# Queries on the column halves as outer and middle 256, and one sum of exponentials instead of two in front of its product

## The chip, the core and the metric

The kernel runs on one core of a Trainium2 chip. The core has a matrix engine (TensorE, called PE; PEld is its loading of weights), VectorE (DVE), ScalarE (ACT), GpSimd (POOL) and SyncE (SP), each with a queue of its own that runs in order, and 16 DMA engines. The metric is the device time of one execution in microseconds (us); lower is better.

## The reference

One step of an encoder layer over 2048 prompt tokens and 32 sample tokens with a width of 1024. A combined projection gives the columns of three groups of heads: two recurrences, and a forgetting attention with 8 heads of 64 numbers. Their outputs are joined and go through an output projection; a feed-forward block with 2816 hidden numbers follows. All arrays are float32. The change is in the prompt's attention:

```python
s = jnp.einsum('bqhd,bkhd->bhqk', q, k) * FOX_SCALE
bias = jnp.swapaxes(c_q, 1, 2)[..., :, None] - jnp.swapaxes(c_k, 1, 2)[..., None, :]
s = jnp.where(k_pos[None, :] <= q_pos[:, None], s + bias, -jnp.inf)
return jnp.einsum('bhqk,bkhd->bqhd', jax.nn.softmax(s, axis=-1), v)
```

`c` is the running sum of the log forget values. A query sees the keys up to its own place.

## The kernel before

The prompt's attention is done in 32 *units*: one head `h` and one group `g` of 512 queries, with `g` from 0 to 3. A unit has two generators. `first` loads and splits queries and keys, and `shift` finds each query's largest score: matmuls L665 into a PSUM bank, maxima on DVE (L667, and L670 with a mask for the last piece), a small matmul L677 that turns them into a row, L680 and L681. `second` calls `values`, which the diff touches.

`values` goes over blocks of 128 keys, 4g+4 of them. For each, two matmuls (L728, L729) give the scores transposed, with keys on the partitions and 512 queries along the columns; the last four blocks are on the diagonal, where block j has no use for the first 128j queries (`c0`) and gets a mask added on DVE (L732). ACT takes the exponential (L738) into a tile `pt`; for the first two blocks this tile is one of two accumulators `acc[0]`, `acc[1]`. Four blocks at a time, `use` multiplies the value rows with `pt` (L712). The value block is 64 columns wide, half of PE's array, so the 512 queries are cut in two: x=0 is queries 0 to 255 and writes PSUM partitions 0 to 63, x=1 is queries 256 to 511 and writes partitions 64 to 127 of the bank `pv`. Each float32 matmul of this line appears in the trace as two rows with a weight load each. In the group with the diagonal the last block is multiplied first. In group 0, whose first four blocks are the diagonal, the order is that of the blocks. `use` also adds `pt` to the accumulator of the block's parity (L722), on POOL or DVE by the block's number (`FX_POOL`); the trace calls the accumulators `fx_acc`.

At the end `quotient` multiplies a matrix of ones with both accumulators (L827; four matmuls, each half accumulating over two), which puts each query's sum of exponentials on all 64 partitions. After that come a logarithm and an exponential on ACT (L832, L833), a product on DVE that reads the bank (L834), and two stores to the array `yT` from ACT's queue (L836), one per half. The output projection reads `yT` later.

The order in which generators advance is written out in `run` (a time for `first` and one for `second`, with a lead between them) and in `paced`, which mixes the attention with the other work: the last projection of the inputs and the loading of the output weights for group 0, then the output projection of the first four token tiles (L1739 to L1741) and the first feed-forward block (L1881 to L1883, L1831 to L1833), whose weights are cast on ACT (L1767) and split on POOL (L1768). With one `pv` bank, `run` finishes the unit's quotient at once, `drain(ends.pop(0))`; for some units of group 0 there are two banks and the quotient comes during the next unit. From this program the tile framework's planner makes the final order of each engine's queue ahead of time: it takes the earliest instruction whose inputs it reckons to be ready, and gives L712 a higher priority.

Of the kernel before, what the change touches and what calls it, by code (L numbers as in the profile page):

```python
# [12 lines left out]
AF = mybir.ActivationFunctionType  # L13
ALU = mybir.AluOpType
# [546 lines left out]
class Fox:  # L561
# [123 lines left out]
    def values(self, k, q, nq, blocks, vr, hc, dst, done, pp):  # L685

        nc, fp = self.K.nc, self.fp
        ka, kb = k  # L690
        qa, qb = q
        nx = 2 if nq > 256 else 1
        W = nq // nx
        pv = pp("pv")
        acc = [fp.tile([128, 512], F32, name=f"fx_acc{i}", bufs=2) for i in range(2)]
        last = len(blocks) - 1
        todo = []

        def use(n):


            now = [todo.pop(0) for _ in range(n)]
            opens = now[0][0] == 0
            order = now if opens and now[-1][2] else now[::-1]
            mms = [(i, m, pt, x, max(c0, W * x), W * x + W) for i, m, c0, pt in order for x in range(nx)]
            mms = [t for t in mms if t[4] < t[5]]
            left = [sum(t[3] == x for t in mms) for x in range(nx)]
            before = None
            with self.K.tc.high_priority():
                for i, m, pt, x, a, b in mms:  # L710
                    left[x] -= 1
                    mm = nc.tensor.matmul(pv[64 * x:64 * x + 64, a - W * x:W], lhsT=vr[:m, i, hc], rhs=pt[:m, a:b],  # L712
                                          start=(opens and i == order[0][0]), stop=(now[-1][0] == last and not left[x]),
                                          skip_group_check=True)
                    if before is not None:
                        self.K.tc.add_manual_dep(mm.ins, before.ins.name, mybir.DependencyInfo(
                            mybir.DependencyClass.NoSync, mybir.DependencyReason.DATA), reason="together")
                    before = mm
            for i, m, c0, pt in now:
                if i >= 2:  # L720
                    eng = nc.gpsimd if i % 8 in FX_POOL else nc.vector
                    eng.tensor_tensor(acc[i % 2][:m, c0:nq], acc[i % 2][:m, c0:nq], pt[:m, c0:nq], ALU.add)  # L722

        for i, (key, m, c0, diag) in enumerate(blocks):
            ks = slice(key, key + m)
            s0 = min(c0, max(0, nq - 256))
            ps = pp("ps")
            nc.tensor.matmul(ps[:m, s0:nq], lhsT=ka[:, ks], rhs=qa[:, s0:nq], start=True, stop=False)  # L728
            nc.tensor.matmul(ps[:m, s0:nq], lhsT=kb[:, ks], rhs=qb[:, s0:nq], start=False, stop=True)  # L729
            if diag:  # L730
                d = min(128, nq - c0)
                nc.vector.tensor_tensor(ps[:m, c0:c0 + d], ps[:m, c0:c0 + d], self.mask_t[:m, :d], ALU.add)  # L732
            pt = acc[i] if i < 2 else fp.tile([128, 512], F32, name="fx_pt", bufs=FX_PT)
            if i < 2 and c0:
                nc.gpsimd.memset(pt[:, :c0], 0.0)
            if i < 2 and m < 128:
                nc.gpsimd.memset(pt[:, :nq], 0.0)
            nc.scalar.activation(pt[:m, c0:nq], ps[:m, c0:nq], AF.Exp)  # L738
            todo.append((i, m, c0, pt))
            if len(todo) == FX_LAG + FX_TOGETHER:  # L740
                use(FX_TOGETHER)
            yield
        while todo:
            use(min(len(todo), FX_TOGETHER))
            yield
        done(self.quotient(acc, pv, nq, nx, dst))

    def sample(self, g, pp):

# [68 lines left out]
                            in_=r[:64, 128:256].rearrange("d (h t) -> d h t", h=4))  # L818
        yield

    def quotient(self, acc, pv, nq, nx, dst):


        nc, W = self.K.nc, nq // nx
        for i in range(2):
            for x in range(nx):
                nc.tensor.matmul(pv[64 * x:64 * x + 64, 256:256 + W], lhsT=self.ones, rhs=acc[i][:, W * x:W * x + W],  # L827
                                 start=(i == 0), stop=(i == 1), skip_group_check=True)
        yield
        r, P = acc[0], 64 * nx  # L830
        s = r[:P, 256:256 + W]
        nc.scalar.activation(s, pv[:P, 256:256 + W], AF.Ln)  # L832
        nc.scalar.activation(s, s, AF.Exp, scale=-1.0)  # L833
        nc.vector.tensor_tensor(r[:P, :W], pv[:P, :W], s, ALU.mult)  # L834
        for x in range(nx):
            nc.scalar.dma_start(out=dst(x), in_=r[64 * x:64 * x + 64, :W])  # L836

    def run(self, units, nk, slots, pp, lead):


        K, nc, fp = self.K, self.K.nc, self.fp
        vs, ks, ends = {}, {}, []
# [8 lines left out]
        def load_v(p):  # L851
            NB = nk // 128
            o = len(vs) % slots * NB
            vs[p] = self.vr[:, o:o + NB, :]
            nc.sync.dma_start(out=vs[p], in_=K.tm[:nk, 128 * p:128 * p + 128].rearrange("(b t) c -> t b c", t=128))
# [14 lines left out]
        def second(u, h, g):  # L870
            row, hc = 256 + 64 * h, slice(64 * (h % 2), 64 * (h % 2) + 64)
            if h // 2 not in vs:
                load_v(h // 2)
            blocks = [(128 * b, 128, max(0, 128 * b - 512 * g), b >= 4 * g) for b in range(4 * g + 4)]
            yield from self.values(ks[h], u["q"], 512, blocks, vs[h // 2], hc, lambda x: K.yT[
                row:row + 64, 512 * g + 256 * x:512 * g + 256 * x + 256], ends.append, pp)

        units = [(h, g, {"i": i}) for i, (h, g) in enumerate(units)]
        seen = set()
# [11 lines left out]
        while s < len(units):  # L891
            if gf is None and f < len(units) and s >= need[f]:
                h, g, u = units[f]
                gf = first(u, h, g)
            if gs is None and s < f:
                h, g, u = units[s]
                gs, k = second(u, h, g), 0
            if gs is None or (gf is not None and tf <= ts + lead):
                tf += FX_F
                if next(gf, StopIteration) is StopIteration:  # L900
                    gf, f = None, f + 1
            else:
                ts += 1.0
                k += 1
                if k > FX_END and ends and next(ends[0], StopIteration) is StopIteration:
                    ends.pop(0)
                if next(gs, StopIteration) is StopIteration:
                    gs, s = None, s + 1
                    while ends and len(pp.slots["pv"]) == 1:
                        drain(ends.pop(0))  # L910
            yield
# [1319 lines left out]
```

## Time and profile before

| what | us |
|---|---|
| three timed runs | 3605.97, 3607.12, 3612.27; median 3607.12 |
| the profiled execution, its own time | 3604.76 |
| its span, first to last instruction | 3603.0 |
| granted PE clock over the span | 0.976 of full |

The median of the runs is the time that counts. The trace is of the profiled execution; its span leaves out 1.8 us around the first and the last instruction. Times of day below are us from the span's start. "x" before a number is a count of instructions, and an arrow points at what an instruction writes, from what it reads.

### The profile page before, as it was taken

The page shows a single profiled execution, that of the slowest core. Times are in us where ns is not written, and L with a number is a line of the kernel's source. Part 1 is how long each engine was busy: PE and PEld are TensorE (multiplying, and loading weights), DVE is VectorE, ACT ScalarE, POOL GpSimd, SP SyncE. Part 2 cuts the span into 40 slices and gives each one's busy share as a digit, 9 for nine tenths or more (in the row PEclk, how much of TensorE's full clock was granted, in tenths as well). Part 3 has the DMA queues.
Part 4 walks back from the last instruction along what each step waited for, and adds up shares of the span by engine and source line. Part 5 has one row for each costly group of instructions (what it writes and reads, how often), then busy time and mean ns, then how long its engine had stood idle before and what let it go on. Part 6 is the DMA issues. An engine that isn't in the chain of part 4 may idle for free.

```text
span 3603.0 us, 60961 instructions
## 1 busy us (share of the span) xinstructions
PE 3408.2 (95%) x24106; PEld 2859.4 (79%) x24106; DVE 1883.4 (52%) x3855; ACT 1403.1 (39%) x2865; POOL 1371.8 (38%) x1458
## 2 busy tenths in 40 slices
PE   7999999999999989999999998999999999999999
PEld 5888898877778856666666666779999998998998
DVE  3466667656576555656656655533333344333336
ACT  4356456554555454444434433312222223111212
POOL 5434445434344314544444333333233243222223
PEclk9999999999999979999999999999999999999999
DMA  6433343425532453322222214533222232211212
GB/s 210 144 122 109 99 146 112 126 80 159 186 96 92 129 147 108 92 73 79 77 64 66 58 55 128 181 118 90 65 71 65 70 106 89 65 59 52 66 59 97
DMA packets 362481, 361.24 MB, mean 100 GB/s; under 512 B 35359, under 2 KB 304244, under 8 KB 361140
## 3 DMA queue, kind: packets, MB, share of 16 engines
q1 hardware_dynamic: 324336, 320.02, 29.2%
q10 hardware_dynamic: 37476, 37.29, 3.4%
q8 instruction: 189, 3.10, 0.4%
q14 instruction: 96, 0.79, 0.1%
q0 software_dynamic: 384, 0.05, 0.0%
HBM read 291.14 MB, written 66.14 MB: 99 GB/s over the span
## 4 chain that ended last, share of the span: by engine, by line
PE 61%; DVE 6%; POOL 4%; ACT 3%; DMA 3%; issue 3%; ACTq 0%; SPq 0%; POOLq 0%; DVEq 0%
PE ff_p L1883 8%; PE ff_p L1882 8%; PE ff_p L1881 8%; PE ff_o L1832 4%; PE ff_o L1833 4%; PE ff_o L1831 4%; PE pb_pv L712 4%; PE rw_ps L227 3%; PE pb_sc L665 2%; PE pb_ps L728 2%; PE op_p L1740 1%; PE op_p L1739 1%; PE op_p L1741 1%; PE pb_ps L729 1%; PE ip_p L378 1%
## 5 line engine op out<-in xcount | busy, mean ns | idle before, releaser
L1882 PE MATMUL ff_p<-h_lo,wih 128*128 128x384 f32 (+2 forms) x1760 | 623.0, 354 | 0.1
L1883 PE MATMUL ff_p<-h_hi,wil 128*128 128x384 f32 (+2 forms) x1760 | 621.4, 353 | 1.1 <-POOL wil L1768 1.1
L1881 PE MATMUL ff_p<-h_hi,wih 128*128 128x384 f32 (+2 forms) x1760 | 620.7, 353 | 1.4 <-DVE op_r L1743 0.4
L1768 POOL TENSOR_TENSOR wil<-ff_st,wih 128x1024 fp32r<-128x1024 f32 x134 | 322.4, 2407 | 579.9 <-ACT wih L1767 546.6
L378 PE MATMUL ip_p<-h_hi,w_hi 128*128 128x256 f32 (+1 forms) x1472 | 454.8, 309 | 22.4 <-DVE ip_e L343 9.6
L379 PE MATMUL ip_p<-h_lo,w_hi 128*128 128x256 f32 (+1 forms) x1472 | 423.5, 288 | 5.1 <-POOL h_lo L203 2.0
L380 PE MATMUL ip_p<-h_hi,w_lo 128*128 128x256 f32 (+1 forms) x1472 | 423.4, 288 | 0.4 <-POOL w_lo L336 0.4
L1881 PEld LDWEIGHTS ff_p<-h_hi,wih 128*128 128x128 f32 x1760 | 331.2, 188 | 17.3 <-DVE ff_sg L1812 0.8
L1883 PEld LDWEIGHTS ff_p<-h_hi,wil 128*128 128x128 f32 x1760 | 333.0, 189 | 14.4 <-POOL wil L1768 1.4
L1882 PEld LDWEIGHTS ff_p<-h_lo,wih 128*128 128x128 f32 x1760 | 331.8, 188 | 14.4 <-POOL h_lo L1956 0.6
L378 PEld LDWEIGHTS ip_p<-h_hi,w_hi 128*128 128x128 f32 x1472 | 282.1, 192 | 51.5 <-issue 15.9
L1768 POOL TENSOR_TENSOR wol<-ff_st,woh 128x1024 fp32r<-128x1024 f32 x66 | 162.8, 2471 | 410.0 <-ACT woh L1767 410.0
L722 POOL TENSOR_TENSOR fx_acc<-fx_acc,fx_pt 128x512 f32<-128x512 f32 (+3 forms) x176 | 208.6, 1201 | 262.1 <-PE pb_pv L712 146.8
L1890 DVE TENSOR_TENSOR ff_sg<-ff_sg,ff_p 128x384 f32<-128x384 f32 (+2 forms) x110 | 64.5, 586 | 456.9 <-PE ff_p L1883 456.1
L1837 DVE TENSOR_TENSOR acc<-acc,ff_o 128x512 f32<-128x512 f32 (+1 forms) x306 | 208.8, 684 | 172.9 <-PE ff_o L1833 172.4
L1831 PE MATMUL ff_o<-woh,act_h 128*128 128x512 f32 (+1 forms) x724 | 287.2, 397 | 9.6 <-ACT act_h L1891 7.0
L379 PEld LDWEIGHTS ip_p<-h_lo,w_hi 128*128 128x128 f32 x1472 | 282.6, 192 | 13.4 <-issue 5.1
L1833 PE MATMUL ff_o<-woh,act_l 128*128 128x512 f32 (+1 forms) x724 | 287.9, 398 | 0.0
L1832 PE MATMUL ff_o<-wol,act_h 128*128 128x512 f32 (+1 forms) x724 | 287.6, 397 | 0.0
L380 PEld LDWEIGHTS ip_p<-h_hi,w_lo 128*128 128x128 f32 x1472 | 282.0, 192 | 5.0 <-issue 3.3
L1767 ACT ACTIVATE wih<-ff_st 128x1024 fp32r<-128x1024 f32 x134 | 142.0, 1060 | 365.3 <-PE ff_p L1882 306.2
L336 POOL TENSOR_TENSOR w_lo<-w_st,w_hi 128x256 fp32r<-128x256 f32 (+2 forms) x220 | 164.3, 777 | 172.3 <-ACT w_hi L334 170.3
(450 smaller groups left out, 7042.9 us busy)
## 6 DMA issues: line engine op xcount, KB each, us to landing
ff_st<-w_ffn_in SPq DMA_DIRECT2D x132, 512.0 KB
w_st<-w_in SPq DMA_DIRECT2D x88, 512.0 KB
ff_st<-w_ffn_out SPq DMA_DIRECT2D x68, 512.0 KB
cm<-ip_e SPq DMA_DIRECT2D x92, 256.0 KB
x_t<-w_ada SPq DMA_DIRECT2D x32, 512.0 KB
fx_kr<-cm SPq DMA_DIRECT2D x80, 128.0 KB
w_st<-w_in SPq DMA_DIRECT2D x16, 520.0 KB
w_a<-w_ada SPq DMA_DIRECT2D x8, 1024.0 KB
```

What stands on the lines that cost most here:

```text
L378: nc.tensor.matmul(ps[:, :T], lhsT=whi[:, d, us], rhs=S.hi[:, d, :T], start=(d == 0), stop=False)
L379: nc.tensor.matmul(ps[:, :T], lhsT=whi[:, d, us], rhs=S.lo[:, d, :T], start=False, stop=False)
L380: K.behind[1:] = [nc.tensor.matmul(ps[:, :T], lhsT=wlo[:, d, us], rhs=S.hi[:, d, :T], start=False, stop=(d == ND - 1))]
L722: eng.tensor_tensor(acc[i % 2][:m, c0:nq], acc[i % 2][:m, c0:nq], pt[:m, c0:nq], ALU.add)
L1768: nc.gpsimd.tensor_tensor(lo, st, f32(hi), ALU.subtract)
L1831: nc.tensor.matmul(ps[:m], lhsT=ah[:, js], rhs=wh[:, cs], start=(n == 0), stop=False)
L1832: nc.tensor.matmul(ps[:m], lhsT=ah[:, js], rhs=wl[:, cs], start=False, stop=False)
L1833: nc.tensor.matmul(ps[:m], lhsT=al[:, js], rhs=wh[:, cs], start=False, stop=(n == 1))
L1837: nc.vector.tensor_tensor(acc[j][:m, cs], acc[j][:m, cs], ps[:m], ALU.add)
L1881: nc.tensor.matmul(ps[:, :S], lhsT=w[0][:, ds], rhs=hh[:, d, :S], start=(d == 0), stop=False)
L1882: nc.tensor.matmul(ps[:, :S], lhsT=w[0][:, ds], rhs=hl[:, d, :S], start=False, stop=False)
L1883: nc.tensor.matmul(ps[:, :S], lhsT=w[1][:, ds], rhs=hh[:, d, :S], start=False, stop=(d == ND - 1))
```

## The change

The columns of a unit's 512 queries are dealt out to the halves of the array in another way: half 0 gets the outer ones, 0 to 127 and 384 to 511, and half 1 the middle ones, 128 to 383. A new helper `part` takes these columns out of a tile or an array. On the diagonal, half 0 gets both of its runs for block 0 and only the later run for blocks 1 to 3; half 1 gets 256 columns for blocks 0 and 1, 128 for block 2 and none for block 3.

Before the quotient, POOL adds the second accumulator to the first; the ones are then multiplied with that one sum, once per half. The stores write the outer half as two runs of 128 queries. `values` gets the place to store to as one array instead of a function.

```diff
--- before.py
+++ after.py
@@ -689,8 +689,7 @@
         nc, fp = self.K.nc, self.fp
         ka, kb = k
         qa, qb = q
-        nx = 2 if nq > 256 else 1
-        W = nq // nx
+        nx, part = 2, self.part
         pv = pp("pv")
         acc = [fp.tile([128, 512], F32, name=f"fx_acc{i}", bufs=2) for i in range(2)]
         last = len(blocks) - 1
@@ -702,14 +701,21 @@
             now = [todo.pop(0) for _ in range(n)]
             opens = now[0][0] == 0
             order = now if opens and now[-1][2] else now[::-1]
-            mms = [(i, m, pt, x, max(c0, W * x), W * x + W) for i, m, c0, pt in order for x in range(nx)]
-            mms = [t for t in mms if t[4] < t[5]]
+            mms = [(i, m, pt[:m], x, max(c0, 128 if x else 0)) for i, m, c0, pt in order for x in range(nx)]
+            mms = [t for t in mms if not (t[3] and t[4] >= 384)]
             left = [sum(t[3] == x for t in mms) for x in range(nx)]
             before = None
             with self.K.tc.high_priority():
-                for i, m, pt, x, a, b in mms:
+                for i, m, pt, x, c0 in mms:
                     left[x] -= 1
-                    mm = nc.tensor.matmul(pv[64 * x:64 * x + 64, a - W * x:W], lhsT=vr[:m, i, hc], rhs=pt[:m, a:b],
+                    out, rhs = pv[64 * x:64 * x + 64], part(pt, x)
+                    if x:
+                        out, rhs = out[:, c0 - 128:256], pt[:, c0:384]
+                    elif c0:
+                        out, rhs = out[:, 128:256], pt[:, 384:]
+                    else:
+                        out = out[:, :256].rearrange("p (a b) -> p a b", b=128)
+                    mm = nc.tensor.matmul(out, lhsT=vr[:m, i, hc], rhs=rhs,
                                           start=(opens and i == order[0][0]), stop=(now[-1][0] == last and not left[x]),
                                           skip_group_check=True)
                     if before is not None:
@@ -743,7 +749,8 @@
         while todo:
             use(min(len(todo), FX_TOGETHER))
             yield
-        done(self.quotient(acc, pv, nq, nx, dst))
+        nc.gpsimd.tensor_tensor(acc[0], acc[0], acc[1], ALU.add)
+        done(self.quotient(acc[0], pv, dst))
 
     def sample(self, g, pp):
 
@@ -818,22 +825,26 @@
                             in_=r[:64, 128:256].rearrange("d (h t) -> d h t", h=4))
         yield
 
-    def quotient(self, acc, pv, nq, nx, dst):
-
-
-        nc, W = self.K.nc, nq // nx
-        for i in range(2):
-            for x in range(nx):
-                nc.tensor.matmul(pv[64 * x:64 * x + 64, 256:256 + W], lhsT=self.ones, rhs=acc[i][:, W * x:W * x + W],
-                                 start=(i == 0), stop=(i == 1), skip_group_check=True)
+    def part(self, t, x):
+
+
+        return t[:, 128:384] if x else t.rearrange("p (a b) -> p a b", b=128)[:, 0:4:3, :]
+
+    def quotient(self, acc, pv, dst):
+
+
+        nc, W = self.K.nc, 256
+        for x in range(2):
+            nc.tensor.matmul(pv[64 * x:64 * x + 64, W:2 * W], lhsT=self.ones, rhs=self.part(acc, x), start=True, stop=True,
+                             skip_group_check=True)
         yield
-        r, P = acc[0], 64 * nx
-        s = r[:P, 256:256 + W]
-        nc.scalar.activation(s, pv[:P, 256:256 + W], AF.Ln)
+        s = acc[:, W:]
+        nc.scalar.activation(s, pv[:, W:2 * W], AF.Ln)
         nc.scalar.activation(s, s, AF.Exp, scale=-1.0)
-        nc.vector.tensor_tensor(r[:P, :W], pv[:P, :W], s, ALU.mult)
-        for x in range(nx):
-            nc.scalar.dma_start(out=dst(x), in_=r[64 * x:64 * x + 64, :W])
+        nc.vector.tensor_tensor(acc[:, :W], pv[:, :W], s, ALU.mult)
+        for x in range(2):
+            r = acc[64 * x:64 * x + 64, :W]
+            nc.scalar.dma_start(out=self.part(dst, x), in_=r if x else r.rearrange("p (a b) -> p a b", b=128))
 
     def run(self, units, nk, slots, pp, lead):
 
@@ -872,8 +883,8 @@
             if h // 2 not in vs:
                 load_v(h // 2)
             blocks = [(128 * b, 128, max(0, 128 * b - 512 * g), b >= 4 * g) for b in range(4 * g + 4)]
-            yield from self.values(ks[h], u["q"], 512, blocks, vs[h // 2], hc, lambda x: K.yT[
-                row:row + 64, 512 * g + 256 * x:512 * g + 256 * x + 256], ends.append, pp)
+            yield from self.values(ks[h], u["q"], 512, blocks, vs[h // 2], hc, K.yT[
+                row:row + 64, 512 * g:512 * g + 512], ends.append, pp)
 
         units = [(h, g, {"i": i}) for i, (h, g) in enumerate(units)]
         seen = set()
```

## Rows read from the trace of the kernel before

**Rows 1.** The page: busy time of each engine, share of the span, instructions.

```profile
PE 3408.2 (95%) x24106; PEld 2859.4 (79%) x24106; DVE 1883.4 (52%) x3855; ACT 1403.1 (39%) x2865; POOL 1371.8 (38%) x1458
```

**Rows 2.** Windows A:B, length; busy PE, PEld, DVE, ACT, POOL; clock, DMA.

```profile
1231.00:1370.00 139.00, 122.41 (x660) 88.90 (x659) 79.40 (x220) 67.49 (x133) 26.88 (x32) 0.83 0.50 144
1370.00:2190.00 820.00, 769.23 (x3822) 531.63 (x3823) 499.86 (x911) 350.71 (x615) 367.21 (x241) 0.98 0.26 74
```

**Rows 3.** The chain that ended last, 1370 to 2190 us, shares by line.

```profile
by line: PE pb_pv L712 14.3%; PE pb_sc L665 7.7%; PE ff_p L1883 7.0%; PE ff_p L1881 6.9%; PE ff_p L1882 6.9%; PE pb_ps L728 6.7%; PE pb_ps L729 5.3%; issue 5.0%; POOL fx_acc L722 5.0%; PE ff_o L1831 3.8%; PE ff_o L1832 3.7%; PE ff_o L1833 3
```

**Rows 4.** Waits of PE and PEld, 1370 to 2190: us, times, longest.

```profile
PE pb_sc L665 <- DVE fx_mx L667: 19.3, 12, 2.2
...
PEld pb_pv L827 <- issue: 2.5, 11, 0.4
```

**Rows 5.** PE in order of time at a unit's end: start, us, line, form.

```profile
1935.77 0.40 PE L1883 MATMUL ff_p<-h_hi,wil 128*128 128x512 f32 x1
1936.01 0.39 PE L1881 MATMUL ff_p<-h_hi,wih 128*128 128x512 f32 x1
1936.33 1.08 PE L712 MATMUL pb_pv<-fx_pt,fx_vr 128*64 128x128 f32 x9
1937.09 0.38 PE L827 MATMUL pb_pv<-fx_acc,fx_ones 128*64 128x256 f32 x1
1937.24 0.38 PE L712 MATMUL pb_pv<-fx_pt,fx_vr 128*64 128x256 f32 x1
1937.30 0.38 PE L827 MATMUL pb_pv<-fx_acc,fx_ones 128*64 128x256 f32 x1
...
1937.73 1.19 PE L827 MATMUL pb_pv<-fx_acc,fx_ones 128*64 128x256 f32 x5
1938.85 0.50 PE L665 MATMUL pb_sc<-fx_ka,fx_qa 68*128 68x512 f32 x1
```

**Rows 6.** L827: count, ns least/median/most, first and last start, form.

```profile
L827 PE MATMUL pb_pv<-fx_acc,fx_ones x256: 379/379/690, 1247.4 to 2185.3; 128*64 128x256 f32 x128
```

**Rows 7.** PE in order of time: two units of group 0, a later one.

```profile
1246.51 0.65 PE L712 MATMUL pb_pv<-fx_pt,fx_vr 128*64 128x256 f32 x2
...
1268.35 0.43 PE L712 MATMUL pb_pv<-fx_pt,fx_vr 128*64 128x128 f32 x2
1268.72 0.39 PE L378 MATMUL ip_p<-h_hi,w_hi 128*128 128x256 f32 x1
...
1269.62 1.08 PE L827 MATMUL pb_pv<-fx_acc,fx_ones 128*64 128x256 f32 x8
...
1595.54 1.08 PE L827 MATMUL pb_pv<-fx_acc,fx_ones 128*64 128x256 f32 x8
```

**Rows 8.** The sums, line 722, on POOL and on DVE.

```profile
L722 POOL TENSOR_TENSOR fx_acc<-fx_acc,fx_pt x176: 452/1280/2352, 1246.1 to 2182.6; 128x512 f32<-128x512 f32 x112, 128x256 f32<-128x256 f32 x32, 128x128 f32<-128x128 f32 x16, 128x384 f32<-128x384 f32 x16
...
L722 DVE TENSOR_TENSOR fx_acc<-fx_acc,fx_pt x80: 275/1324/2840, 1370.1 to 2183.0; 128x512 f32<-128x512 f32 x56, 128x128 f32<-128x128 f32 x16, 128x384 f32<-128x384 f32 x8
```

**Rows 9.** POOL's next work after rows 5's unit, idle time before it.

```profile
1938.01 2.38 POOL L1768 TENSOR_TENSOR wil<-ff_st,wih 128x1024 fp32r<-128x1024 f32 x1 [1.52 <-ACT wih L1767]
```

**Rows 10.** In order of time, the first unit of group 1 and the next.

```profile
1383.53 0.41 DVE L834 TENSOR_TENSOR fx_acc<-pb_pv,fx_acc 128x256 f32<-128x256 f32 x1
...
1384.33 0.44 PE L712 MATMUL pb_pv<-fx_pt,fx_vr 128*64 128x256 f32 x2
```

**Rows 11.** Two groups of the recurrence's matmuls, on 128 columns each.

```profile
L227 PE MATMUL rw_ps<-rw_G,rw_kb x264: 272/272/386, 189.1 to 1171.4; 64*128 64x128 f32 x132
...
L227 PE MATMUL rw_ps<-rw_kn,rw_tt x264: 269/269/320, 226.5 to 1199.1; 64*64 64x128 f32 x132
```

**Rows 12.** DVE, then POOL, in order of time, around 1901 us.

```profile
1901.31 2.18 DVE L722 TENSOR_TENSOR fx_acc<-fx_acc,fx_pt 128x128 f32<-128x128 f32 x1
...
1900.97 2.37 POOL L1768 TENSOR_TENSOR wil<-ff_st,wih 128x1024 fp32r<-128x1024 f32 x1
```

**Rows 13.** DVE's maxima, line 667: count, ns least/median/most, form.

```profile
L667 DVE TENSOR_REDUCE fx_mx<-pb_sc x192: 673/691/694, 1337.7 to 2158.2; 128x1 f32<-128x512 f32 x192
```

## The prediction

> **What bounds the kernel now.** I read the page first: the matrix engine (PE) is busy for 95% of the span, VectorE (DVE) for 52, POOL for 38 [rows 1]. The change lies in the stretch of the attention's 32 units (8 heads by 4 groups of 512 queries), so I read windows next [rows 2]. The 8 units of group 0 run at 1231 to about 1370 us beside the last input projection and the loading of the output weights, with PE busy 122 of 139 us at a granted clock of 0.83. The 24 other units run at 1370 to 2190 us beside the output projection and the first feed-forward block; there PE is busy 769 of 820 us at 0.98, and POOL only 367. The chain of that second stretch [rows 3] is matmuls for the most part, with POOL's and the issue's 5% each as the largest other pieces. The waits say what ends PE's idle time [rows 4]: scores L665 waiting for the maxima on DVE is the largest with 19 us; the product of the sums, L827, comes far down, with 2.5. So PE time taken out here should come off the end unless it is turned into a wait.
>
> Next, how the column halves work, from one unit's end on PE [rows 5]. L712 (values) and L827 (ones by sums) are 64 columns wide; half x=0 and half x=1 run side by side. Rows of L827 start between rows of L712, each some 0.215 us after the one before it on its own half (1937.09, 1937.30 and, as the fourth, 1937.73). There are 256 rows of L827 [rows 6] for the code's 4x32=128 matmuls, so a matmul is two rows: 256 columns hold a half for 0.43 us, 128 for 0.22. That L827 begins while L712 still runs shows half 0 to be done early: its queries 0 to 255 need fewer of the diagonal blocks. The full-width L665 waits for the slower half.
>
> **The change part by part.** *Values.* On the four diagonal blocks half 0 has 256+128 columns today and half 1 has 256+256+256+128=896. With outer and middle queries each has 640. The group ends when the slower half does, so it becomes 256 columns, 0.43 us, shorter. That holds where the four blocks run together, as in [rows 5]: 24 units, 10.3 us. In group 0 blocks 2 and 3 come apart from the others and each alone, as pairs of rows of 256 and of 128 columns [rows 7]; only block 2 is halved (two rows of 256 on one half become two of 128 on both), 0.22 us in 8 units, 1.7 us. One more matmul of 128 columns is issued per unit; it lies on the half that was idle.
>
> Whether that gain is whole depends on half 1 not waiting for its turn: the last block, issued first, now has work for half 0 alone. The rows above, where half 0 runs ahead of half 1, say that it needn't. The Trainium skill ("TensorE: Matmul & The Clock Gate", The mechanism) says the opposite, that matmuls start and end in strict issue order; L827, emitted after all of L712, starting before its last rows is not what that describes. By the rule half 1 would idle for half 0's first 0.22 us in 24 units, and the sum below would be 5.2 us smaller; I go by the rows.
>
> *The product.* Two matmuls on each half become one: 0.43 us in 32 units, 13.7 us. **Together 25.7 us of PE.**
>
> *The add on POOL.* A 128x512 add there has a median of 1.28 us over mixed shapes, most of them this one [rows 8]; 32 of them are 41 us on an engine that is idle for over half of the stretch [rows 2]. What counts is that L827 now waits for it. In [rows 5] the product follows the values at once. POOL's last add for that unit ends at 1938.01-1.52=1936.49, and POOL is idle from there to 1938.01 [rows 9], so the sum would be there at about 1937.8; the shortened values would be through at 1936.33+1.08=1937.41. If nothing stood between, PE would wait some 0.4 us. But PE's order is fixed beforehand by a planner that fills such waits. In [rows 7] it put projection matmuls between the values of 1268.35 and the product of 1269.62, and in 6 of the 32 units the product stands apart already (first at 1269.62, last at 1595.54). The feed-forward block always has matmuls ready. I take it that the product is put some 1.3 us later and that other matmuls fill most of the time.
>
> What the filling costs: a change between full-width and half-width work. In [rows 5] the full-width pitch is 0.24 us (1935.77 to 1936.01) but 0.32 lies before the first L712, and 0.31 instead of 0.215 follows the last L827: about 0.09 each, 0.18 for leaving and coming back, in the 26 units where values and product are together now: 4.7 us. Where the filling misjudges, PE waits. Nothing (all filled) and 0.4 us in each of 32 units (none, by rows 5) bound it at 0 to 13 us; later last adds make it more, which is a rival below. I take 5, nearer to the filled end.
>
> *What is queued behind.* On POOL the add waits for the last sums of both accumulators, one of which may be DVE's, and behind it stand L1768's weight splits; with POOL idle for over half of the stretch [rows 2] I charge nothing. The accumulator pair has two buffers, and the one PSUM bank of a unit is free later by about 1.4 us. After most units the next values come many us later; in two they follow at once (L834 at 1383.53 plus 0.41, next L712 at 1384.33 [rows 10], and alike in the very first unit): 2 us in all.
>
> *The rest* is nothing: the two stores keep their bytes, the outer half's now in two runs of 128 numbers, and what reads `yT`, the output projection, comes much later. The outer half's moving columns come in two runs of 128. The recurrence has matmuls with a moving side in two runs of 64: 0.272 us a row against 0.269 for one run of 128 [rows 11]. Those 0.003 for the 512 rows of half 0 that become so would be 1.5 us if half 0 were always the slower; I take nothing.
>
> **Sum:** -25.7+4.7+5+2=-14 us. The profiled execution took 3604.8 us by its own clock with a span of 3603.0; the three timed runs have a median of 3607.1, 2.4 above it. 3604.8-14=3590.8, as a median **3593 us**.
>
> **The rivals.** *A: the wait takes the gain back.* If the planner leaves the product close behind the values, each unit waits for the add. The wait is 0.4 us in rows 5 and up to a whole add with hand-over, 1.4, where the last sum ends with the values. The middle, 0.9, in 32 units is 28 us against 25.7: about 3609, no change. For it: the product follows the values directly in 26 units. Against: the filled places of rows 7, and the small place of L827 in rows 4.
>
> *B: the add holds up DVE.* A DVE add of two SBUF operands takes 0.28 us at best but 2.18 at 1901.31, all the while L1768 runs on POOL [rows 8, 12]. If each new add did that to an instruction PE waits for, 41 us would come on top of -25.7+4.7: 3625 for the profile, 3627 as a median. It decides once more than 21/1.28, some 16 of the 32 adds, do so. Against: right after a unit DVE works on maxima and masks, which read PSUM; L667 never took over 0.694 us in 192 [rows 13], with POOL busy 45% of the time. Exposed is what joins two SBUF tiles, such as the queries' small part L646. The Trainium skill ("SBUF — State Buffer", SBUF: two separate sides) has it so: DVE with two SBUF inputs and POOL take an exclusive lock on a port pair; rows 12 agree with it (2.18 for 0.28).
>
> *C: everything is filled*, no stall and no lost latency: -25.7+4.7=-21 us, 3586; without the changes of width 3581.
>
> *D: the changed order.* The planner's order of thousands of instructions shifts; in this stretch PE waits for DVE's maxima in pieces of up to 2.2 us [rows 4], and four more or fewer of these move the end by some 9 us either way. This widens each case and isn't one by itself.
>
> *E: half 1 waits its turn* behind half 0's first matmul of the diagonal, 0.22 us in 24 units: 5.2 us less gain, 3598. The order of starts in rows 5 speaks against it.
>
> **How the numbers follow.** No change can be told from this kernel's measurement within 0.2%, 7.2 us: 3599.9 to 3614.3. Chances: my sum 0.40, E 0.08, C 0.20, A 0.22, B 0.10. My sum and E, with D, fall within 0.2% in 0.06 and C is always faster; A is faster in 0.05, slower in 0.03; B is slower in 0.08. Faster 0.67, same 0.22, slower 0.11. The range goes from C's 3581, a little under it for D leaves out 0.07, up to A with its later waits, 3612, which leaves out 0.12. The likeliest case's own range is 3586 to 3600.
>
> **What would show it.** L827 with 128 rows for 256, L712 with 64 more rows and no L827 between its rows; the group of 12 L712 rows some 0.4 us shorter in 1370 to 2190; 32 new POOL adds of about 1.3 us; matmuls of another line between values and product in most units; PE busy in the attention's stretch down by 20 us or more. Wrong would be: PE waits put down to POOL's add of 20 us or more (A), L667 or L670 starting late behind a long DVE instruction beside the new add (B), or the 128-column rows of L712 starting more than 0.11 us apart on a half.

## The result and the profile after

The changed kernel took **3614.76 us** (median of 13 runs, 3608.39 to 3622.22), the kernel before, run on the same chip, 3606.45 (13 runs, 3601.68 to 3613.23). The ratio is 1.0022 with a 95% interval of 1.0013 to 1.0030: slower by 0.2%, where I had forecast 3593 us and faster. The profiled execution took 3614.76 us with a span of 3613.0, against 3604.76 and 3603.0 before.

Line numbers grow by 6 to 11: L712 is now L718, L722 L728, L827 L838, L834 L844, L1768 L1779, L1881 to L1883 L1892 to L1894; the new add on POOL is L752. First the page's busy times, which answer to [rows 1].

```profile
PE 3396.6 (94%) x24042; PEld 2851.2 (79%) x24042; DVE 1877.6 (52%) x3855; ACT 1404.2 (39%) x2865; POOL 1416.8 (39%) x1490
```

PE has 11.6 us less work, in a span that is 10.0 us longer: it stands idle some 22 us more. The windows of [rows 2]:

```profile
1231.00:1370.00 139.00, 119.25 (x640) 86.71 (x639) 80.21 (x220) 66.95 (x131) 35.07 (x40) 0.81 0.49 141
1370.00:2190.00 820.00, 749.90 (x3692) 519.38 (x3691) 494.87 (x905) 347.25 (x604) 393.04 (x257) 0.96 0.25 73
```

In the same 820 us PE gets through 3692 matmul rows instead of 3822 (some 48 of the 130 are rows that the change itself takes away, two per unit), at a clock of 0.96 instead of 0.98. What it waits for is in the list of waits, 1370 to 2190 us (us in total, times, longest), which answers to [rows 4]:

```profile
PE pb_sc L665 <- DVE fx_mx L667: 23.3, 14, 2.5
PEld pb_pv L838 <- POOL fx_acc L752: 23.0, 17, 5.0
...
POOL fx_acc L752 <- DVE fx_acc L728: 19.4, 13, 4.6
PE pb_pv L838 <- POOL fx_acc L752: 15.9, 15, 4.5
```

The product, 2.5 us in [rows 4], now stands beside the scores' wait for the maxima, which stays the largest (48.0 us at the scores' weight loads, not shown). Over the whole trace, the view of one line gives counts, ns least/median/most, and what its engine (PE and PEld together) sat idle for; it answers to [rows 6]. Of L718, the values, the same view has the rows' counts.

```profile
L838 PE MATMUL pb_pv<-fx_acc,fx_ones x128: 379/430/688, 1248.1 to 2205.6; 128*64 128x256 f32 x128
its engine sat idle before it (us, times) until:
  POOL fx_acc L752: 55.3, 47
```

```profile
L718 PE MATMUL pb_pv<-fx_pt,fx_vr x960: 272/379/690, 1246.0 to 2205.2; 128*64 128x256 f32 x143, 128*64 128x128 f32 x49
```

```profile
L752 POOL TENSOR_TENSOR fx_acc<-fx_acc,fx_acc x32: 1255/1276/1758, 1246.8 to 2203.2; 128x512 f32<-128x512 f32 x32
```

So the parts themselves are as forecast: 128 rows of the product for 256, 64 more rows of values, 32 adds of 1.28 us. Of the 55.3 us, 23.0 are PE's own (22 times) and 32.3 are the same waits as its weight loads saw them; that the list above has 23.0 for PEld in a shorter stretch is chance. A unit's end in order of time, PE and then POOL, is to be read beside [rows 5] and [rows 9]; the brackets hold the idle time before and its releaser.

```profile
1954.03 0.40 PE L1893 MATMUL ff_p<-h_lo,wih 128*128 128x512 f32 x1
1954.55 1.35 PE L718 MATMUL pb_pv<-fx_pt,fx_vr 128*64 128x128 f32 x14
1956.91 0.65 PE L838 MATMUL pb_pv<-fx_acc,fx_ones 128*64 128x256 f32 x4 [1.01 <-POOL fx_acc L752]
1957.49 0.50 PE L665 MATMUL pb_sc<-fx_ka,fx_qa 68*128 68x512 f32 x1
```

```profile
1954.57 0.46 POOL L728 TENSOR_TENSOR fx_acc<-fx_acc,fx_pt 128x128 f32<-128x128 f32 x1 [1.07 <-ACT fx_pt L744]
1955.11 1.75 POOL L752 TENSOR_TENSOR fx_acc<-fx_acc,fx_acc 128x512 f32<-128x512 f32 x1
```

Values, nothing, product: no other matmul lies between, and PE stands for 1.01 us until the add is through. Going through PE's rows in order, I find that so in 19 of the 24 units of groups 1 to 3; the others have 1, 1, 1, 4 and 41 rows between. Even where nothing holds the add up, 1.40 us pass from the end of the last addition to the product. The worst unit shows what else there is; POOL stands last.

```profile
1779.00 1.35 PE L718 MATMUL pb_pv<-fx_pt,fx_vr 128*64 128x128 f32 x14
1784.86 1.12 PE L838 MATMUL pb_pv<-fx_acc,fx_ones 128*64 128x256 f32 x4 [4.51 <-POOL fx_acc L752]
1785.91 0.80 PE L1892 MATMUL ff_p<-h_hi,wih 128*128 128x512 f32 x1
1786.51 0.63 PE L1893 MATMUL ff_p<-h_lo,wih 128*128 128x512 f32 x1
...
1788.46 0.39 PE L1892 MATMUL ff_p<-h_hi,wih 128*128 128x512 f32 x1
```

```profile
1781.21 2.38 POOL L1779 TENSOR_TENSOR wol<-ff_st,woh 128x1024 fp32r<-128x1024 f32 x1
1783.56 1.25 POOL L752 TENSOR_TENSOR fx_acc<-fx_acc,fx_acc 128x512 f32<-128x512 f32 x1
```

The last addition ended at 1781.40 (DVE, not shown), but a weight split of 2.38 us had just begun on POOL and the add stood behind it. That happened in two of the 32 units. And PE doesn't only lose the 4.51 us: afterwards a row takes 0.63 us for 0.39. The granted clock says why (windows, columns as in [rows 2]):

```profile
1770.00:1780.00 10.00, 10.00 (x66) 6.75 (x62) 7.22 (x11) 6.09 (x11) 9.84 (x6) 1.00 0.19 56
...
1785.00:1790.00 5.00, 5.00 (x17) 3.45 (x18) 1.11 (x2) 2.56 (x6) 0.00 (x0) 0.68 1.08 292
1790.00:1800.00 10.00, 8.06 (x33) 6.07 (x32) 7.87 (x15) 1.90 (x3) 2.38 (x1) 0.92 0.44 127
```

From 2.4 GHz throughout (1.00) it goes to 0.68 on average, partly at 1.2 GHz, once PE has stood for 4.51 us. After the 1.01 us of the unit above the rows kept their lengths.

### The profile page after: what moved, and what is told of

Same layout as the page of the kernel before. It is cut to its first block, busy times and chain, and to the rows that moved or that the text cites. A ratio compares the mean times of both kernels' runs of the same rounds, so it can differ in the third digit from the quotient of the medians.

```text
span 3613.0 us, 60923 instructions
## 1 busy us (share of the span) xinstructions
PE 3396.6 (94%) x24042; PEld 2851.2 (79%) x24042; DVE 1877.6 (52%) x3855; ACT 1404.2 (39%) x2865; POOL 1416.8 (39%) x1490
## 5 line engine op out<-in xcount | busy, mean ns | idle before, releaser
L1892 PE MATMUL ff_p<-h_hi,wih 128*128 128x384 f32 (+2 forms) x1760 | 622.7, 354 | 0.9 <-DVE op_r L1754 0.4
L1894 PE MATMUL ff_p<-h_hi,wil 128*128 128x384 f32 (+2 forms) x1760 | 621.6, 353 | 1.1 <-POOL wil L1779 1.1
L1779 POOL TENSOR_TENSOR wil<-ff_st,wih 128x1024 fp32r<-128x1024 f32 x134 | 324.8, 2424 | 559.6 <-ACT wih L1778 538.6
L1892 PEld LDWEIGHTS ff_p<-h_hi,wih 128*128 128x128 f32 x1760 | 331.8, 189 | 18.4 <-issue 1.9
L1894 PEld LDWEIGHTS ff_p<-h_hi,wil 128*128 128x128 f32 x1760 | 333.9, 190 | 14.6 <-POOL wil L1779 1.4
L1779 POOL TENSOR_TENSOR wol<-ff_st,woh 128x1024 fp32r<-128x1024 f32 x66 | 159.9, 2427 | 401.6 <-ACT woh L1778 401.6
L728 POOL TENSOR_TENSOR fx_acc<-fx_acc,fx_pt 128x512 f32<-128x512 f32 (+3 forms) x176 | 207.7, 1194 | 237.5 <-ACT fx_pt L744 115.7
```

The source lines that it names most:

```text
L1779: nc.gpsimd.tensor_tensor(lo, st, f32(hi), ALU.subtract)
L1892: nc.tensor.matmul(ps[:, :S], lhsT=w[0][:, ds], rhs=hh[:, d, :S], start=(d == 0), stop=False)
L1894: nc.tensor.matmul(ps[:, :S], lhsT=w[1][:, ds], rhs=hh[:, d, :S], start=False, stop=(d == ND - 1))
```

## The experiments

The theories: **W**, the product waits for POOL's add, and that alone turns the gain into a loss; **D**, dealing the queries in outer and middle costs something itself; **P**, the add hurts by holding POOL or VectorE, not by being waited for; **O**, the planner's other order. A ratio is against the kernel before on the same chip, with its 95% interval. Each run's account is a window from 1231 us to the 289th matmul of the output projection: by then all have done the same attention, and PE's idle time is the length less the busy time. Rows of waits are for 1231 to 2210 us where no other stretch is named. Before, then after:

```profile
1231.00:2290.00 1059.00, 977.41 (x4980) 684.57 (x4980) 636.56 (x1201) 453.05 (x810) 415.28 (x284) 0.95 0.32 93
```

```profile
1231.00:2300.00 1069.00, 966.97 (x4917) 676.61 (x4917) 635.26 (x1202) 455.48 (x810) 458.43 (x316) 0.95 0.31 92
```

81.6 us idle have become 102.0, and the busy time, which should have fallen by 25.7, fell by 10.4.

**The halves alone.**

```diff
-        nc.gpsimd.tensor_tensor(acc[0], acc[0], acc[1], ALU.add)
-        done(self.quotient(acc[0], pv, dst))
+        done(self.quotient(acc, pv, dst))
...
+        for i in range(2):
+            for x in range(2):
+                nc.tensor.matmul(pv[64 * x:64 * x + 64, W:2 * W], lhsT=self.ones, rhs=self.part(accs[i], x),
+                                 start=(i == 0), stop=(i == 1), skip_group_check=True)
```

> Only the dealing is kept: queries as outer and middle 256, the product still multiplies ones with both accumulators in turn (four matmuls), no add on POOL. Theory W (the loss is the product's wait for POOL's add; the dealing itself gains what was forecast for it, 24 x 0.43 + 8 x 0.22 = 12 us of TensorE): 3589 to 3600 us, no value-to-product wait for POOL, first out-projection weights cast at the times of before within 3 us. Theory D (the dealing itself costs, by strided moving data, a half that waits its turn, or stores of two runs): 3610 to 3620. Theory O (only a chance order of the planner lost the time): anything within 10 us of before, with the landmarks between the in-projection's end and the feed-forward's start moved by either sign.

Measured: **3593.26 us**, ratio 0.9965 (0.9952 to 0.9978), by the ratio 12.6 us faster than before, where 12.0 had been worked out. The account, and the product's largest wait in it:

```profile
1231.00:2280.00 1049.00, 961.57 (x5046) 682.10 (x5047) 628.16 (x1204) 456.32 (x814) 414.64 (x287) 0.96 0.32 94
```

```profile
PE pb_pv L838 <- POOL fx_acc L728: 1.3, 3, 0.7
```

D falls: the dealing is worth what its count says. That half 1 doesn't wait its turn can be read from the starts of the rows in the trace of the changed kernel. The 14 rows at 1954.55 us begin with a matmul of half 0 alone; this is PE from 1954.50 to 1954.57 us:

```profile
1954.55 0.34 PE L718 MATMUL pb_pv<-fx_pt,fx_vr 128*64 128x128 f32 x2
```

Two rows have started, though on one half the next row would come 0.16 us after the first: the second is half 1's. In all 24 units of groups 1 to 3 the second start of these rows lies 13 or 14 ns behind the first. The Trainium skill ("TensorEngine Tiling (Array Packing)", Key Properties) has the tiles of the array operate independently; by that half 1 needn't wait for half 0, and these starts agree.

**The add alone**, on the old dealing: the diff is the new POOL line and one matmul for two on each half.

> Only the add is made: queries dealt as before in two runs of 256, POOL adds the two accumulators and one product per half follows. Theory W: the 32 products save 13.7 us of TensorE but wait for POOL, and group 0's units between the in-projection's end and the out-projection's start come later and push the output weights back: 3612 to 3628 us, PE and PEld idle for POOL's add 20 us or more in all. Theory D: the add is not what costs, 3592 to 3602. Theory O: within 10 us of before, of either sign, and no sum of the two parts to the whole.

Measured: 3609.95 us, ratio 1.0015 (1.0003 to 1.0027). The wait is there, though shorter than in the whole change:

```profile
PE pb_pv L827 <- POOL fx_acc L746: 12.8, 12, 2.5
```

The sign is W's, a little below its numbers. But the time is within 10 us of before, and the parts don't add: -12.6 and +5.4 make -7, the whole is +8. That is what O expected, so this run doesn't decide between W and O. From here to the whole change the wait grows from 12.8 to 23.0 us. The shorter values bring the product sooner to the same add, and the order differs too: here one to three matmuls stand between values and product in 12 of the 24 later units, in the whole change some stand there in 5. How much each of the two does isn't shown.

**No add, and an add that nobody waits for.** Two kernels, one without the add, one in which POOL adds the second accumulator to itself. In both the product reads the first accumulator alone, so it is also spared the wait for the second's last addition; in the halves alone, which read both without an add, PE waited 1.3 us for such additions, so little hangs on that.

```diff
-        nc.gpsimd.tensor_tensor(acc[0], acc[0], acc[1], ALU.add)
+        nc.gpsimd.tensor_tensor(acc[1], acc[1], acc[1], ALU.add)
         done(self.quotient(acc[0], pv, dst))
...
-        nc.scalar.activation(s, pv[:, W:2 * W], AF.Ln)
+        nc.scalar.activation(s, pv[:, W:2 * W], AF.Ln, bias=self.K.eps_c[:, 3:4])
```

> The changed kernel without the add: the product takes the first accumulator alone, so the odd key blocks are left out of the denominator, and 1 is added to it inside the logarithm so that it is never zero. All of TensorE's saving, no add and no wait for one. Theory W: 3578 to 3592 us (3606 less the 25.7 us of the sum, back up to 13 us for the cover that before's matmuls gave to the waits for exponentials). Theory D: 3600 or more.

> As the run without the add (odd key blocks left out of the denominator, 1 added to it), but POOL makes an add of the same size, of the second accumulator to itself, that no product reads. POOL's and the SBUF's load is that of the changed kernel, the wait is gone. Theory W: within 4 us of the run without the add. Theory P (POOL's add hurts by holding VectorE's additions or by coming ahead of other work on POOL, rather than by being waited for): 10 us or more above the run without the add, near 3610.

Measured: 3580.12 us, ratio 0.9931 (0.9915 to 0.9947), and 3583.97, ratio 0.9939 (0.9924 to 0.9955). Of the second, the account, the product and the add:

```profile
1231.00:2269.00 1038.00, 948.91 (x4917) 670.95 (x4918) 633.08 (x1204) 459.59 (x815) 453.17 (x321) 0.96 0.33 95
```

```profile
L838 PE MATMUL pb_pv<-fx_acc,fx_ones x128: 378/380/689, 1249.5 to 2174.0; 128*64 128x256 f32 x128
```

```profile
L752 POOL TENSOR_TENSOR fx_acc<-fx_acc x32: 1037/1040/1539, 1249.9 to 2171.6; 128x512 f32<-128x512 f32 x32
```

P falls: 33 us of such adds on POOL change the time by 3.9 us, and the two intervals overlap. **With the product made to wait for the add, the kernel takes 3614.8-3584.0=31 us more**, and these two kernels have the same 4917 rows on PE up to that point: after is 12.9 us more idle and 18.1 us longer busy on them. The product's median is 430 ns in the one and 380 in the other. Much of both lies in the stretch where the planner mixes the first four of the 24 later units with the output projection (after, then the unwaited add; from the end of group 0 to the end of the fourth):

```profile
1341.00:1521.00 180.00, 155.49 (x698) 109.14 (x699) 104.61 (x197) 77.52 (x126) 87.64 (x60) 0.90 0.38 117
```

```profile
1341.00:1503.00 162.00, 143.22 (x695) 103.35 (x696) 98.05 (x188) 74.70 (x122) 84.84 (x60) 0.95 0.41 125
```

About as many rows take 12 us more at a clock of 0.90 for 0.95. But these 18 us are hardly the wait itself. Of PE's 23.0 us of waiting for the add only 3.4 lie in this stretch, and the scores' wait for the maxima has grown more, from 2.4 us to this:

```profile
PE pb_sc L665 <- DVE fx_mx L667: 9.2, 6, 2.1
PE pb_pv L838 <- POOL fx_acc L752: 3.4, 2, 2.7
```

The first of these two waits for the add begins at 1477.7 us, and the clock was down long before: 0.66 from 1371 to 1381 and from 1391 to 1401 us, where the other kernel has 1.00. The run "Group 0 exempt" below has the same add in these four units, with 4.4 us of waiting, and takes 167 us for them. So 18 of the 31 us are not the wait's own length. They may come with the other order, as O has it; why this stretch is slow in after stays open. Group 0 doesn't count: it ends at 1341 us in both, though in the change PE waits 7.1 us for the add there. The other 13 us lie in the last 20 units, where PE waits 12.5 us for the add, and in the other kernel 0.9 for an addition (after, then the unwaited add):

```profile
1521.00:2208.00 687.00, 637.91 (x3191) 440.06 (x3190) 418.89 (x765) 288.96 (x510) 324.07 (x209) 0.98 0.23 67
```

```profile
1503.00:2177.00 674.00, 633.17 (x3195) 441.34 (x3194) 419.49 (x765) 290.86 (x510) 319.05 (x210) 0.98 0.24 68
```

The kernel without any add takes 679 us for them, so the 13 are uncertain by some 5. W is borne out in that the gain is there once nothing waits for the add; that the wait alone makes the loss isn't shown.

**A longer wait.** A second POOL instruction between add and product:

```diff
         nc.gpsimd.tensor_tensor(acc[0], acc[0], acc[1], ALU.add)
+        nc.gpsimd.tensor_tensor(acc[0], acc[0], self.K.eps_c[:, 3:4].broadcast_to([128, 512]), ALU.mult)
```

> The changed kernel with a second instruction on POOL between the add and the product (the sum times one, 128 x 512). If the product waits in place, each of the 32 waits grows by up to 1.3 us less what the planner puts ahead of the product for it. Theory W: 3622 to 3655 us. Rival O (the place that the planner gave the product by chance, not the wait's length, makes the loss): within 6 us of the changed kernel, 3609 to 3621.

Measured: 3656.51 us, ratio 1.0144 (1.0127 to 1.0161), just above W's range and far from O's.

```profile
1231.00:2340.00 1109.00, 981.51 (x4916) 684.09 (x4916) 650.48 (x1204) 456.62 (x814) 498.51 (x355) 0.93 0.30 89
```

```profile
PE pb_pv L839 <- POOL fx_acc L753: 42.0, 24, 5.0
```

O falls as the whole cause. This kernel's last unit ends after 2210 us; with it the wait is 44.9 us. So PE's wait for POOL is 1.8 us (for an earlier addition), 23.0 and 44.9, and the time 3584, 3615 and 3657. Clearer is the count in the last 20 units alone, where all three do the same work. The wait there is 0.9, 12.5 and 27.6 us and the length 674, 687 and, with the second POOL instruction, 709 us:

```profile
1534.00:2243.00 709.00, 641.04 (x3159) 437.02 (x3158) 423.59 (x761) 286.20 (x507) 346.61 (x229) 0.96 0.23 65
```

The first 12 us of wait go with 13 us, the next 15 with 22, at a clock of 0.96 for 0.98.

**Group 0 exempt**, `if last < 4: done(self.quotient(acc, pv, dst))`, and the add only for the other groups:

> The changed kernel, but the eight units of group 0 keep ones with both accumulators and have no add on POOL; groups 1 to 3 as changed. Theory G (most of the loss comes from group 0, in the stretch with no other matmuls, and from the output weights that it sets back): 3592 to 3600 us, the weights' casts at the times of before within 3 us. Theory S (the loss is made unit by unit in the groups 1 to 3, whose products wait too): 3605 to 3613.

Measured: 3626.84 us, ratio 1.0062 (1.0039 to 1.0084). G falls: group 0 ends no sooner, at 1344 us, and the value is above S's range too. Its wait, in the 24 units that still add:

```profile
PE pb_pv L842 <- POOL fx_acc L755: 18.8, 17, 4.5
```

In the same 24 units the changed kernel waits 15.9 us, so the wait there isn't less. The profiled run of it (3617.2 us) is the fastest of its six, so the trace shows less than the median. Why it is some 12 us slower than the changed kernel is open.

**The add on VectorE**, `nc.vector` for `nc.gpsimd`:

> The changed kernel with the add on VectorE in place of POOL. Theory W: the add takes some 0.7 us for POOL's 1.27 and is behind no other work of POOL, so about half of the 31 us that the wait costs comes back: 3594 to 3604 us. Rival V (VectorE's queue is as late as POOL's, since it holds the additions, the reductions of the next unit's scores and the feed-forward's work in order): 3608 or more.

Measured: 3612.95 us, ratio 1.0015 (1.0001 to 1.0029): V's time, but not its mechanism.

```profile
PE pb_pv L838 <- DVE fx_acc L752: 16.7, 10, 3.8
```

VectorE's queue isn't late: in every unit the add begins within 0.8 us of the last addition, and 27 of the 32 adds take 0.7 us. The other five, each beside a weight split on POOL, take 2.64 to 2.81 us, and 13.2 of the 16.7 us of waiting stand behind them. One of them, POOL and then VectorE:

```profile
1637.73 2.33 POOL L1779 TENSOR_TENSOR wol<-ff_st,woh 128x1024 fp32r<-128x1024 f32 x1
1637.79 2.81 DVE L752 TENSOR_TENSOR fx_acc<-fx_acc,fx_acc 128x512 f32<-128x512 f32 x1 [2.07 <-POOL fx_acc L728]
```

That is the hold of [rows 12], which rival B described: an add of two SBUF tiles that began 0.06 us after the split's start was through 0.5 us after the split's end.

**The add sooner:**

```diff
-                    eng.tensor_tensor(acc[i % 2][:m, c0:nq], acc[i % 2][:m, c0:nq], pt[:m, c0:nq], ALU.add)
+                    r = acc[i % 2 if last < 4 or i < last - 3 else 0]
+                    eng.tensor_tensor(r[:m, c0:nq], r[:m, c0:nq], pt[:m, c0:nq], ALU.add)
+                if i == last - 4:
+                    nc.gpsimd.tensor_tensor(acc[0], acc[0], acc[1], ALU.add)
...
-        nc.gpsimd.tensor_tensor(acc[0], acc[0], acc[1], ALU.add)
-        done(self.quotient(acc[0], pv, dst))
+        done(self.quotient(acc[:1] if last > 3 else acc, pv, dst))
```

> The changed kernel, but in the groups 1 to 3 POOL's add of the two accumulators comes ahead of the additions of the unit's last four blocks, all of which then go into the first accumulator; the units of group 0 have no add and take ones with both accumulators. The product then ends a chain of four narrowing additions and not an add of 512 columns behind them. Theory W (only the wait for the late add costs): 3576 to 3592 us, which is the run of the halves alone less up to 24 x 0.43 us. Rival C (the chain of additions into one accumulator is as long as the add that it replaces, 512, 384, 256 and 128 columns one after the other over two engines): 3600 or more, with the product's wait now put down to the additions.

Measured: 3635.23 us, ratio 1.0085 (1.0066 to 1.0104): C, and worse than the change.

```profile
PE pb_ps L737 <- ACT fx_pt L747: 23.1, 10, 5.7
...
PE pb_pv L841 <- DVE fx_acc L729: 6.3, 5, 2.5
```

The product's wait is down to 6.3 us, but PE now waits 23.1 us for the exponentials, 5.6 before in such rows. It isn't their buffers, for which ScalarE waits 1.0 us. VectorE's first addition of the last four blocks stands until POOL's add (L731) is through, the masks of the diagonal (L741) stand behind it in VectorE's queue, and the exponentials wait for the masks. Eight of the nine waits of over 1 us follow that chain; in the longest, PE stood 5.66 us behind this:

```profile
2117.40 0.69 DVE L729 TENSOR_TENSOR fx_acc<-fx_acc,fx_pt 128x512 f32<-128x512 f32 x1 [3.72 <-POOL fx_acc L731]
2118.01 0.49 DVE L741 TENSOR_TENSOR pb_ps<-pb_ps,fx_mask_t 128x128 f32<-128x128 f32 x2
2118.33 0.77 ACT L747 ACTIVATE fx_pt<-pb_ps 128x384 f32<-128x384 f32 x2 [6.60 <-DVE pb_ps L741]
```

**The product later.** First in the program only; its place there moved behind the next unit's first three score blocks, the bank taken no sooner than its first use:

```diff
...
+                while k == 4 and ends and len(pp.slots["pv"]) == 1:
+                    drain(ends.pop(0))
                 if next(gs, StopIteration) is StopIteration:
                     gs, s = None, s + 1
-                    while ends and len(pp.slots["pv"]) == 1:
-                        drain(ends.pop(0))
```

> The changed kernel, but where one PSUM bank serves the values (groups 1 to 3) the product and what follows it stand in the program behind the next unit's first three score blocks and directly ahead of its first values, and not directly behind the unit's own last values. Theory W: the score matmuls cover the add and the wait goes: 3582 to 3598 us. Rival L (the bank comes free later, and the next unit's values and so its exponentials' buffers wait for it): 3605 or more, with the first values of the units waiting for VectorE's multiplication.

Measured: 3612.73 us, ratio 1.0009 (0.9996 to 1.0022). Neither mechanism: the planner put the product back, and in the last 20 units PE's rows show no matmul or one between values and product. In group 0 it did move: 12 to 62 rows stand between in its first five units.

```profile
PE pb_pv L841 <- POOL fx_acc L755: 14.3, 17, 2.5
```

Then in TensorE's own order too, with no add and both accumulators in group 0; the second of these has `k == 2`. The lines above act in group 0 as well, so its products aren't where they were: 12 to 59 rows stand ahead of them in five of its units, and 36 to 38 in three with `k == 2`.

```diff
...
+                    self.K.tc.add_manual_dep(mm.ins, self.score.ins.name, mybir.DependencyInfo(
+                        mybir.DependencyClass.NoSync, mybir.DependencyReason.DATA), reason="later")
```

> Groups 1 to 3 have the add on POOL, and the product is held in TensorE's own order behind the score matmuls of the next unit's third block (an order without a semaphore); the eight units of group 0 keep ones with both accumulators and no add. Theory W (the loss is the product standing a few matmuls too early in TensorE's queue): the wait for POOL's add falls under 3 us and the time to 3580 to 3595 us. Rival L (the one PSUM bank of the values comes free later, the next unit's first values and then its exponentials' six buffers wait): 3600 to 3640, with waits of the values for VectorE's multiplication or of the scores for ScalarE's exponentials in the wait's place.

> As the run before it, but the product is held behind the score matmuls of the next unit's first block only, two blocks sooner. Theory W: 3580 to 3592 us, not above the run with the third block. Rival L: better than that run by what the bank comes free sooner, but still 3597 or more.

Measured: 3612.56 us, ratio 1.0016 (1.0003 to 1.0030), and 3623.40, ratio 1.0044 (1.0031 to 1.0058). Of the first, waits:

```profile
PE pb_ps L738 <- ACT fx_pt L748: 15.0, 12, 3.5
...
PE pb_pv L846 <- POOL fx_acc L732: 3.3, 2, 2.6
```

The wait for the add is gone from both, as W's first half said (0.7 and 0.3 us are left; the 3.3 in the list are group 0's, for its ordinary additions), and the gain did not come. L holds for the time, but its mechanism isn't in the trace: the values wait 0.4 us for VectorE's multiplication and ScalarE 1.1 for an exponentials' buffer. The scores do wait 15.0 us for the exponentials (7.1 with the unwaited add), and VectorE stands 46.0 us at the quotient's multiplication until ScalarE's exponential is there (14.1 in the change). Whether that is what takes the gain isn't shown, and why holding the product for less is worse, against what L said, stays open.

## Why the prediction was wrong

**The halves and the product: right.** The values' 12.0 us were 12.6, and with the product's 13.7 the sum of 25.7 was 22 to 26 in the two kernels without the wait. E, the turn-taking, would have made the halves alone 5.2 us less worth, near 3599; their interval, 3589 to 3598, ends just below, and the starts of the rows, 13 or 14 ns apart where E needs 0.22 us, rule it out.

**The step that failed: "I take it that the product is put some 1.3 us later and that other matmuls fill most of the time".** Its term was +5 us, with bounds 0 and 13; with the 4.7 and the 2 that were charged beside it, all that the add would bring was put at 11.7. In its place the runs show 31, the change against the unwaited add. Four things in it were wrong. I took the filling from [rows 7], whose first units lie beside the input projection; in groups 1 to 3 the product stays where it stood, directly behind the values in 19 of 24 units, though feed-forward matmuls follow it closely, and PE waited 23.0 us in 22 units. I priced the wait from one unit [rows 5, 9], in which POOL's last addition was early and POOL was idle: but the add itself waits for DVE's last addition (20.5 us in 14 units) or, in two units, stands behind a weight split, which my "I charge nothing" passed over. I charged a wait at its own length, which the last 20 units bear out for the first 12 us of it and not for the next 15. And D, the changed order, had no term in the sum and some 9 us of width: 18 of the 31 us lie in the first four units after group 0, where PE waited 3.4 us for the add, and 12 of these are busy time at a clock of 0.90 for 0.95. What slowed that stretch stays open.

The small place of L827 in [rows 4] said nothing of this: it was the wait of a product whose sums were ready. Rival A, at 0.22, had the mechanism, the product close behind the values. That its 28 us lie near the 31 is luck in part: it counted 0.9 us of waiting in each of 32 units, PE waited 23.0 us in all, and 18 of the 31 lie where it hardly waited.

**B** falls for this change: the unwaited add costs some 4 us, and that within the noise. The hold itself is real, as the add on VectorE showed. In the unit shown the add itself took 1.75 us, beside a VectorE instruction on two SBUF operands (L646, 0.69 us) that had started 0.06 us sooner. Over all 32 adds it is the later of two such neighbours that is held: the 11 adds that began while L646 or L634 ran took 1.58 to 1.76 us, and the ten L646 and L634 that began during an add took 1.00 to 1.80 us for the usual 0.67 to 0.69. **C**'s 3581 to 3586 is what the two kernels without a wait reached, 3580 and 3584, but with nothing filled: they have no wait to fill. **D**, the changed order, isn't told apart from the wait by these runs: six kernels that keep the add and move it, its engine or its product lie between 3612 and 3635 us, their waits for it don't order them, and the same four units took 180 us in the change and 167 in one of the six with the same add. The charges of 4.7 us for changes of width and 2 us for the bank were not measured by themselves.

The fastest of all runs that keep the whole computation is the halves alone, 3593.26 us, faster than both kernels.

## What to carry to other kernels

An instruction that moves work from the busiest engine to an idle one is worth its saving only if the busy engine's order has something else at that place: look at what stands directly ahead of the consumer in that order, and at the latest of all the producer's inputs, not at the idle share of the producer. Where a planner fixes the order, take its filling only from places with the same work beside them. And split a change in two before judging it: here one half was worth 12.6 us, and the other took back more than both had gained.

## What was not expected

A wait of PE can cost more than its length: in the last 20 units 15 more us of it went with 22 us, and 4.51 us of standing still were followed by rows of 0.63 us for 0.39. The Trainium skill ("TensorE: Matmul & The Clock Gate", Part 1: The HAM clock gate) has the clock halved after idle time and restored by sustained work; the granted clock of 0.68 behind that wait, 1.00 ahead of it, agrees.

The same add on POOL took 1276 ns with two different tiles as operands and 1040 with one tile twice (medians of 32).
